# Fourteen of sixteen column groups of the second MLP product by the seven-product scheme, with sums made by GpSimd

## The chip, the cores and the metric

One core of one Trainium2 chip runs the whole kernel. The time is device time in microseconds, the median over runs; the profile is of one execution. The engines are named as the profile names them: PE is TensorE's matmul and PEld its weight load, DVE is VectorE, ACT ScalarE, POOL GpSimd, SP SyncE, on whose queue all of this kernel's loads and stores stand.

## The reference

One layer of an encoder on 512 tokens of 2048 features, all in float32. A projection feeds sixteen heads of two recurrent kinds (gated linear recurrence and gated delta rule), their output is projected back and added to x, and then comes the part that this change is about:

```python
h2 = rmsnorm(x, norm2_w[layer])
hid = jnp.square(jax.nn.relu(jnp.einsum("btd,df->btf", h2, w_mlp_in[layer])))
x = x + jnp.einsum("btf,fd->btd", hid, w_mlp_out[layer])
...
return rmsnorm(x, final_norm_w)
```

Here hid has 512 x 8192 elements and w_mlp_out 8192 x 2048. The last line but one is the second MLP product.

## The kernel before

**Precision.** Every float32 operand of a large product is split into a high part, rounded by ACT to the matmul's float32 format (`fp32r`), and a low part, the rest, subtracted by DVE. A product is then three matmuls (mm3, lines 103 to 106: high x high, high x low, low x high). So each tile of weights costs one ACT copy and one DVE subtraction before PE can use it.

**The second product (from line 1189 on).** The 64 row tiles (128 rows each) of w_mlp_out make four blocks of 16 (`FB`, `NB`), and each block is taken through four groups of 512 columns. A group has eight steps (`NK`); a step takes a pair of row tiles. After each group the result is added to x2, which lies in DRAM and is loaded before (`load_group`) and stored after (`store_group`), through one buffer on chip.

A *plain* group (`plain_group`, line 1254) does 2 row tiles x 4 token tiles x 3 = 24 matmuls of 512 columns per step. Its weights are 512 KB from DRAM into a raw buffer (three of them), one ACT copy, one DVE subtraction (lines 75 and 78).

A *fast* group (`fast_group`, line 1293) uses Strassen's scheme in Winograd's form: halves of the tokens, even and odd row tiles, halves of the columns, seven products of half the size for eight. That is 7 x 2 x 3 = 42 matmuls of 256 columns per step, in seven PSUM banks. `weights7` (line 1265) makes a step's weights: the load into a raw buffer, three sums of quarters into a tile of tag "T" (`quarters`, line 1200, two buffers; lines 1273 to 1275: one instruction 512 wide, two of 256), then two splits: b, 768 wide, from raw (lines 1277, 1278), and wh and wl, 1024 wide, from the sums (lines 1282, 1283; three buffers each). `finish_fast` (line 1310) adds the seven banks into x2: one ACT copy and nine DVE additions, of which the first six read a bank and the last three have both inputs on chip in SBUF.

**Left-hand sides.** For each pair of row tiles of a block the hidden activations come back from DRAM in two forms. `load_parts` (line 1211) loads 512 KB into a raw buffer and splits them into hidA, which plain and fast groups use. `load_sums` (line 1220) loads the same 512 KB once more, into a "T" buffer, makes the four sums of the scheme in place, each 256 wide (lines 1226 to 1229), and splits the tile into hidS, which fast groups alone use. There are eight buffers for parts and eight for sums, so those of the next block can be written only as the last group of this one gives them up.

**When they are made.** `todo` (lines 1332 to 1340) puts each load at a step of the program. Parts of block b at step kp + 6 (`LAG`) counted from the start of group 3 of the block before; sums of block b at the group ahead of the block's first fast group. `FAST` names the fast groups of each block: (2, 3) in blocks 0 to 2 and (1, 2) in block 3, eight of sixteen. So the program puts the sums of blocks 0 to 2 into plain group 1 and those of block 3 into plain group 0. The last group of the last block is written apart (lines 1359 to 1405) and is plain.

**Order.** PE's instructions stand in the order of the program (`manual_schedule`, line 265). For the other engines a scheduler sets a fixed order by priority ahead of the run, and each engine and the SP queue then work through it in that order; a waiting instruction holds up all that stand behind it on its engine.

GpSimd has little to do: powers and masks in the first phase, nothing in the second product but four small powers at the end.

Of the kernel before, what the change touches and what calls it, by code (L numbers as in the profile page):

```python
# [16 lines left out]
P = 128  # L17
# [15 lines left out]
def encoder_layer_kernel(ctx, tc, x, norm1_w, w_in, lb_fwd, lb_bwd, hg_norm_w, conv_w,  # L33
# [13 lines left out]
    def after(later, first):  # L47
        """issue order only"""
        tc.add_manual_dep(getattr(later, "ins", later), getattr(first, "ins", first).name,
                          mybir.DependencyInfo(mybir.DependencyClass.NoSync, mybir.DependencyReason.DATA),  # L50
                          reason="issue order")

    # ------------------------------------------------------------------ pools
# [17 lines left out]
    # ------------------------------------------------------------------ weights  # L71
# [11 lines left out]
    def load_cols(w, k0, c0, name):  # L83
        """[1024 rows of w from k-tile k0] x 128 columns -> [128, 8 k-tiles, 128]"""
# [9 lines left out]
    def load_rows(w, k0, c0, name):  # L94
        """[256 rows of w from k-tile k0] x 512 columns -> [128, 2 k-tiles, 512]"""
# [12 lines left out]
    def project(w, c0, rh, rl, name):  # L108
        """(columns c0..c0+127 of act @ w) transposed: PSUM [128 columns, 512 tokens]; four k-tiles per step"""
# [9 lines left out]
    def project_narrow(w, c0, width, rh, rl, name, between):  # L119
        """the same for a few columns; high and low parts of the weights side by side, their products to be added"""  # L120
# [20 lines left out]
    # ------------------------------------------------------------------ input rows  # L141
# [10 lines left out]
    # ------------------------------------------------------------------ constants  # L152
# [61 lines left out]
    # ------------------------------------------------------------------ first norm, transposed  # L214
# [3 lines left out]
    def tiles16(name):  # L218
        """sixteen [128, 512] tiles, four to a unit of 8 KB"""
# [5 lines left out]
    def rms_scale(ss, n, width, name, post=None):  # L225
        """(ss / width + eps) ** -0.5 for [128, n] sums of squares"""
# [43 lines left out]
    # ------------------------------------------------------------------ masks  # L270
    # rows are the partition index p, columns f
# [9 lines left out]
    def tri(dst, src, fill, lower, strict=False):  # L281
        """keep src where f >= p (upper) or f <= p (lower), else fill"""
# [21 lines left out]
    # ------------------------------------------------------------------ decays and betas of the delta rule  # L304
# [7 lines left out]
    def decays():  # L312
# [47 lines left out]
        # summation matrices, [r, t]: which g_r enter the sum of token t  # L360
# [29 lines left out]
    # ------------------------------------------------------------------ centred short convolution + silu  # L390
# [10 lines left out]
    # ------------------------------------------------------------------ delta rule, first pass: N = strict(beta k k^T decay)  # L401
# [13 lines left out]
    def decay_matrix(gb, wa, wb, mask, sign, h):  # L415
        """exp(sign * (gb - w + mask)), in place; w = wa / wb for the columns of a pair's first / second half"""
# [46 lines left out]
    # ------------------------------------------------------------------ delta rule: (I - M)^-1 of 128 blocks of 64 x 64  # L463
# [22 lines left out]
    # ------------------------------------------------------------------ shared end of a head: norm of o, transposed  # L486
    mixh = bp.tile([P, NH, T], F32, tag="B0", name="mixh")

    def head_norm(o, qcol, wcol, dst, name):
        """o [128 tokens, 4 x 128] (PSUM or SBUF) -> dst = (rmsnorm(o * qcol) * w) transposed"""  # L490
# [26 lines left out]
    # ------------------------------------------------------------------ HGRN2 head  # L517
# [14 lines left out]
    def hgrn_gates(h, d, pf, q):  # L532
        """decayed queries and keys of one direction, all [128 channels, 512 tokens]"""
# [31 lines left out]
    def hgrn_extend(h, r, size, dl, name):  # L565
        """decays of qi / ks reach over 2 * size tokens instead of size"""
# [11 lines left out]
    def hgrn_scores_32(h, r):  # L578
        """scores [s, t]: inside blocks of 32 tokens and between the two blocks of each 64"""
# [87 lines left out]
    # ------------------------------------------------------------------ delta rule, second pass  # L667
    def delta_second(h):
# [22 lines left out]
        # merge 64 -> 128  # L691
# [743 lines left out]
```

## Time and profile before

| | us |
|---|---|
| median of 3 runs (2541.36 to 2544.16) | 2541.64 |
| span of the profiled execution, first to last instruction | 2540.0 |
| second MLP product up to its last matmul, from 1856 | 675.3 |
| PE busy in the span | 2504.5 |
| DVE busy in the span | 1744.5 |
| ACT busy in the span | 1213.1 |
| POOL busy in the span | 64.9 |

The time of the profiled execution is known by its span alone; what lies around it shows in the median being 1.6 us longer. In a view that groups instructions a row is line, engine, operation, what it writes and reads, shapes, count | busy time, mean ns of one | idle time of the engine before them and what ended it. Busy time of PE counts matmuls whose ends are modelled and which overlap, so a step's time is read from stretches between starts, not from one matmul's duration. A name such as wl<-wsum,wh gives the tile written and those read, without buffer numbers.

### The profile page before, as it was taken

Reading aid. Unit: us, or ns where it says so; the run is one execution under the profiler, and the core shown is the slowest. Engines: PE = TensorE matmul, PEld = TensorE weight load, DVE = VectorE, ACT = ScalarE, POOL = GpSimd, SP = SyncE. Lnnn points to the kernel's source line nnn. Section 1 sums busy time; section 2 is a strip of 40 time slices with the busy share of each in tenths; the row PEclk is TensorE's granted clock in tenths of the full one; section 3 lists DMA queues with packets and bytes.
Section 4 is the critical chain, followed back from the end, with each engine's and each line's share of the span. In section 5 each row is a group of like instructions: output and inputs, shape, how many; then the busy total and the mean of one; then the engine's idle time right before and its main releaser. Section 6 shows DMA issues by size and latency. Waiting matters only on the chain.

```text
span 2540.0 us, 39593 instructions
## 1 busy us (share of the span) xinstructions
PE 2504.5 (99%) x16010; PEld 2236.5 (88%) x16010; DVE 1744.5 (69%) x2782; ACT 1213.1 (48%) x1768; POOL 64.9 (3%) x94
## 2 busy tenths in 40 slices
PE   7999999999999999999999999999999999999998
PEld 5888888887888888888899999999988989989897
DVE  5989995445545454444777777777767867868885
ACT  5564555563444443344655555555544433434443
POOL 2000000000000100000000000000000000000000
PEclk9999999999999999999999999999999999999999
DMA  5662223233333332433333344334375573754764
GB/s 159 176 171 75 75 75 114 83 101 88 108 98 94 103 101 67 166 125 124 127 132 125 129 151 136 125 126 150 111 237 191 184 248 134 264 191 167 245 217 168
DMA packets 339452, 359.50 MB, mean 142 GB/s; under 512 B 42898, under 2 KB 256052, under 8 KB 334148
## 3 DMA queue, kind: packets, MB, share of 16 engines
q1 hardware_dynamic: 339268, 356.96, 43.7%
q8 instruction: 126, 2.06, 0.3%
q14 instruction: 58, 0.48, 0.1%
HBM read 306.55 MB, written 50.36 MB: 141 GB/s over the span
## 4 chain that ended last, share of the span: by engine, by line
PE 88%; DMA 4%; DVE 4%; ACT 2%; issue 1%; SPq 0%; ACTq 0%; POOLq 0%; POOL 0%; DVEq 0%
PE mo L106 3%; PE mo L104 3%; PE mo L105 3%; PE p L104 3%; PE p L105 3%; PE p L106 3%; PE wo L104 2%; PE wo L106 2%; PE wo L105 2%; PE mc L104 2%; PE mc L106 2%; PE md L104 2%; PE md L106 2%; PE mc L105 2%; PE md L105 2%; PE ma L104 2%
## 5 line engine op out<-in xcount | busy, mean ns | idle before, releaser
L1099 ACT ACTIVATE wh<-s 128x1024 fp32r<-128x1024 f32 x128 | 135.8, 1061 | 130.2 <-PE mb L105 48.7
L105 PE MATMUL mo<-wl_mo,hidA 128*128 128x512 f32 x480 | 187.4, 390 | 1.8 <-DVE wl_mo L78 1.8
L104 PE MATMUL mo<-wh_mo,hidA 128*128 128x512 f32 x480 | 188.5, 393 | 0.7 <-DVE u L1316 0.3
L106 PE MATMUL mo<-wh_mo,hidA 128*128 128x512 f32 x480 | 188.2, 392 | 0.0
L1100 DVE TENSOR_TENSOR wl<-s,wh 128x1024 fp32r<-128x1024 f32 x128 | 156.6, 1223 | 36.7 <-ACT wh L1099 36.6
L1099 ACT ACTIVATE wh<-praw 128x1024 fp32r<-128x1024 f32 x96 | 101.9, 1061 | 148.5 <-PE mc L105 52.3
L1100 DVE TENSOR_TENSOR wl<-praw,wh 128x1024 fp32r<-128x1024 f32 x96 | 117.1, 1220 | 36.6 <-ACT wh L1099 36.4
L1277 ACT ACTIVATE wb<-raw 128x768 fp32r<-128x768 f32 x64 | 54.1, 845 | 133.3 <-issue 58.1
L105 PEld LDWEIGHTS mo<-wl_mo,hidA 128*128 128x128 f32 x480 | 90.1, 188 | 22.7 <-DVE wl_mo L78 3.1
L105 PE MATMUL p<-wl,hidS 128*128 128x256 f32 x384 | 108.3, 282 | 0.9 <-DVE wl L1283 0.9
L104 PE MATMUL p<-wh,hidS 128*128 128x256 f32 x384 | 108.4, 282 | 0.8 <-DVE x L1355 0.8
L104 PEld LDWEIGHTS mo<-wh_mo,hidA 128*128 128x128 f32 x480 | 90.2, 188 | 21.0 <-DVE x L1316 1.2
L106 PE MATMUL p<-wh,hidS 128*128 128x256 f32 x384 | 108.2, 282 | 0.0
L106 PEld LDWEIGHTS mo<-wh_mo,hidA 128*128 128x128 f32 x480 | 90.1, 188 | 19.7
L1092 DVE TENSOR_TENSOR s<-praw 128x1024 f32<-128x1024 f32 x64 | 78.4, 1225 | 36.3 <-DMA praw<-in_w_mlp_in_dram 35.2
L78 DVE TENSOR_TENSOR wl_wo<-raw_wo,wh_wo 128x1024 fp32r<-128x1024 f32 x32 | 39.2, 1225 | 92.1 <-ACT wh_wo L75 92.1
L104 PE MATMUL wo<-wh_wo,mh 128*128 128x512 f32 x256 | 100.1, 391 | 0.0
L78 DVE TENSOR_TENSOR wl_mo<-raw_mo,wh_mo 128x1024 fp32r<-128x1024 f32 x60 | 73.1, 1220 | 39.2 <-ACT wh_mo L75 39.0
L106 PE MATMUL wo<-wh_wo,ml 128*128 128x512 f32 x256 | 99.7, 389 | 0.0
L105 PE MATMUL wo<-wl_wo,mh 128*128 128x512 f32 x256 | 99.6, 389 | 0.0
L75 ACT ACTIVATE wh_mo<-raw_mo 128x1024 fp32r<-128x1024 f32 x60 | 62.8, 1052 | 66.6 <-PE mo L106 27.6
L1282 ACT ACTIVATE wh<-wsum 128x1024 fp32r<-128x1024 f32 x64 | 67.1, 1050 | 41.2 <-PE mo L106 25.1
(515 smaller groups left out, 8577.8 us busy)
## 6 DMA issues: line engine op xcount, KB each, us to landing
praw<-in_w_mlp_in_dram SPq DMA_DIRECT2D x64, 1024.0 KB, 8.5
raw<-in_w_mlp_out_dram SPq DMA_DIRECT2D x64, 512.0 KB, 4.0
raw_mo<-in_w_mlp_out_dram SPq DMA_DIRECT2D x60, 512.0 KB, 5.1
raw_wo<-in_w_out_dram SPq DMA_DIRECT2D x32, 512.0 KB, 3.6
hid_d<-r SPq DMA_DIRECT2D x64, 256.0 KB, 4.4
raw_h<-hid_d SPq DMA_DIRECT2D x32, 512.0 KB, 4.2
x<-x_d SPq DMA_DIRECT2D x16, 1024.0 KB, 7.1
sums<-hid_d SPq DMA_DIRECT2D x32, 512.0 KB, 4.7
```

The lines of the kernel that those rows point to most:

```text
L75: op = act.activation(wh, raw, AF.Copy)
L78: op = dve.tensor_tensor(wl, raw, wh.bitcast(F32), ALU.subtract)
L104: pe.matmul(ps, ah, bh, start=start, stop=False, skip_group_check=skip)
L105: pe.matmul(ps, ah, bl, start=False, stop=False, skip_group_check=skip)
L106: return pe.matmul(ps, al, bh, start=False, stop=stop, skip_group_check=skip)
L1092: dve.tensor_tensor(t, x0, x1, op)
L1099: act.activation(wh, src, AF.Copy)
L1100: dve.tensor_tensor(wl, src, wh.bitcast(F32), ALU.subtract)
L1277: act.activation(b[:, 0], r[:, 1:4], AF.Copy)
L1282: act.activation(wh, qf, AF.Copy)
```

## The change

Three things are changed, all in the second product:

- `FAST` names fourteen groups: (1, 2, 3), all four, all four, (0, 1, 2). Plain are left group 0 of block 0 and group 3 of block 3.
- The sums of a block are made at `SUM_LAG` = 4 steps after the start of group 3 of the block before, those of block 0 at the steps of its group 0.
- GpSimd makes the three weight sums of `weights7` and two of the four sums of `load_sums`; DVE keeps the two others and all splits.

```diff
-    FAST = ((2, 3), (2, 3), (2, 3), (1, 2))
+    FAST = ((1, 2, 3), (0, 1, 2, 3), (0, 1, 2, 3), (0, 1, 2))
+    SUM_LAG = 4
...
     def load_sums(fb, kp, first):
...
-        dve.tensor_tensor(q[:, 3], q[:, 1], q[:, 3], ALU.add)
+        pool.tensor_tensor(q[:, 3], q[:, 1], q[:, 3], ALU.add)
         dve.tensor_tensor(q[:, 1], q[:, 1], q[:, 0], ALU.subtract)
-        dve.tensor_tensor(q[:, 0], q[:, 3], q[:, 0], ALU.subtract)
+        pool.tensor_tensor(q[:, 0], q[:, 3], q[:, 0], ALU.subtract)
         dve.tensor_tensor(q[:, 2], q[:, 2], q[:, 0], ALU.subtract)
         split8(s, q)
...
     def weights7(fb, g, kp):
...
-        dve.tensor_tensor(q[:, 0:2], r[:, B12:B12 + 1].to_broadcast([P, 2, HT]), r[:, B11:B22 + 1], ALU.subtract)
-        dve.tensor_tensor(q[:, 2], r[:, B22], q[:, 0], ALU.subtract)
-        dve.tensor_tensor(q[:, 3], r[:, B21], q[:, 2], ALU.subtract)
+        pool.tensor_tensor(q[:, 0:2], r[:, B12:B12 + 1].to_broadcast([P, 2, HT]), r[:, B11:B22 + 1], ALU.subtract)
+        pool.tensor_tensor(q[:, 2], r[:, B22], q[:, 0], ALU.subtract)
+        pool.tensor_tensor(q[:, 3], r[:, B21], q[:, 2], ALU.subtract)
...
-            todo.setdefault((4 * b + FAST[b][0] - 1) * NK + kp, []).append((sums, load_sums, b, kp, b == 0 and kp >= 4))
+            at = kp if b == 0 else (4 * b - 1) * NK + kp + SUM_LAG
+            todo.setdefault(at, []).append((sums, load_sums, b, kp, b == 0 and kp >= 4))
```

In the changed kernel lines from 1198 on are one further down: the sums of `load_sums` are lines 1227 to 1230, the weight sums 1274 to 1276, the splits 1210, 1279 and 1284, the additions of a finish 1317.

The order shows what this moves at the join of block 0 and block 1. Names carry block, group and step, or block and row pair, ahead of a running tile number: wsum0_3_6 are the weight sums of block 0, group 3, step 6; wb and wl the low parts of its two splits; sums1_1 the sum tile of block 1, pair 1; hidS and hidA the splits of sums and parts. DVE before, in the last steps of fast group 3 of block 0:

```order
L1273 TENSOR_TENSOR wsum0_3_7_18867<-raw_0_3_7_18865 128x512
L1274 TENSOR_TENSOR wsum0_3_7_18867<-raw_0_3_7_18865,wsum0_3_7_18867 128x256
L1278 TENSOR_TENSOR wb0_3_6_18811<-raw_0_3_6_18805,wb0_3_6_18811 128x768
L1283 TENSOR_TENSOR wl_0_3_6_18815<-wsum0_3_6_18807,wh_0_3_6_18814 128x1024
L1275 TENSOR_TENSOR wsum0_3_7_18867<-raw_0_3_7_18865,wsum0_3_7_18867 128x256
L1209 TENSOR_TENSOR hidA1_0_18862<-raw_h1_0_18860,hidA1_0_18862 128x1024
L1278 TENSOR_TENSOR wb0_3_7_18871<-raw_0_3_7_18865,wb0_3_7_18871 128x768
L1283 TENSOR_TENSOR wl_0_3_7_18875<-wsum0_3_7_18867,wh_0_3_7_18874 128x1024
```

DVE in the changed kernel, in the same two steps and the first of the next block:

```order
L1279 TENSOR_TENSOR wb0_3_6_19041<-raw_0_3_6_19035,wb0_3_6_19041 128x768
L1228 TENSOR_TENSOR sums1_1_19027<-sums1_1_19027 128x256
L1230 TENSOR_TENSOR sums1_1_19027<-sums1_1_19027 128x256
L1284 TENSOR_TENSOR wl_0_3_6_19045<-wsum0_3_6_19037,wh_0_3_6_19044 128x1024
L1210 TENSOR_TENSOR hidS1_1_19026<-sums1_1_19027,hidS1_1_19026 128x1024
L1210 TENSOR_TENSOR hidA1_0_19092<-raw_h1_0_19090,hidA1_0_19092 128x1024
L1279 TENSOR_TENSOR wb0_3_7_19110<-raw_0_3_7_19104,wb0_3_7_19110 128x768
L1228 TENSOR_TENSOR sums1_2_19096<-sums1_2_19096 128x256
L1284 TENSOR_TENSOR wl_0_3_7_19114<-wsum0_3_7_19106,wh_0_3_7_19113 128x1024
L1230 TENSOR_TENSOR sums1_2_19096<-sums1_2_19096 128x256
L1210 TENSOR_TENSOR hidA1_1_19161<-raw_h1_1_19159,hidA1_1_19161 128x1024
L1210 TENSOR_TENSOR hidS1_2_19095<-sums1_2_19096,hidS1_2_19095 128x1024
```

The weight sums have left DVE; between the splits of one step's weights and the next stand two sums, the split of a sum tile and the split of a part. GpSimd in the changed kernel at this place, where it had nothing before:

```order
L1274 TENSOR_TENSOR wsum0_3_6_19037<-raw_0_3_6_19035 128x512
L1227 TENSOR_TENSOR sums1_1_19027<-sums1_1_19027 128x256
L1275 TENSOR_TENSOR wsum0_3_6_19037<-raw_0_3_6_19035,wsum0_3_6_19037 128x256
L1276 TENSOR_TENSOR wsum0_3_6_19037<-raw_0_3_6_19035,wsum0_3_6_19037 128x256
L1229 TENSOR_TENSOR sums1_1_19027<-sums1_1_19027 128x256
L1274 TENSOR_TENSOR wsum0_3_7_19106<-raw_0_3_7_19104 128x512
```

L1229 can start when DVE's L1228 of the same tile is done, and the next step's weight sums stand behind it. The SP queue in the changed kernel, from the load of step 6's weights on:

```order
L1270 DMA raw_0_3_6_19035<-in_w_mlp_out_dram 128x2x512
L1206 DMA raw_h1_0_19090<-hid_d_8722 128x2x512
L1206 DMA sums1_1_19027<-hid_d_8722 128x2x512
L1270 DMA raw_0_3_7_19104<-in_w_mlp_out_dram 128x2x512
L1206 DMA raw_h1_1_19159<-hid_d_8722 128x2x512
L1206 DMA sums1_2_19096<-hid_d_8722 128x2x512
L1270 DMA raw_1_0_0_19200<-in_w_mlp_out_dram 128x2x512
L1206 DMA raw_h1_2_19255<-hid_d_8722 128x2x512
```

Each load of weights stands behind the load of a sum tile. Before, group 3's own weights came ahead of the first sums, and at the join the queue read:

```order
L1269 DMA raw_0_3_7_18865<-in_w_mlp_out_dram 128x2x512
L1205 DMA raw_h1_1_18920<-hid_d_8722 128x2x512
L1205 DMA sums1_0_19261<-hid_d_8722 128x2x512
L98 DMA raw_mo1_0_0_18949<-in_w_mlp_out_dram 128x2x512
L1205 DMA raw_h1_2_18979<-hid_d_8722 128x2x512
L98 DMA raw_mo1_0_1_18984<-in_w_mlp_out_dram 128x2x512
L1205 DMA sums1_1_19300<-hid_d_8722 128x2x512
```

There the weights behind the sums were those of plain steps (raw_mo), which need no "T" buffer.

## The prediction

> **What bounds the kernel now.** I read the page's first part, then stretches of the second MLP product group by group, then PE's waits there.
>
> ```profile
> span 2540.0 us, 39593 instructions
> PE 2504.5 (99%) x16010; PEld 2236.5 (88%) x16010; DVE 1744.5 (69%) x2782; ACT 1213.1 (48%) x1768; POOL 64.9 (3%) x94
> ...
> 1856.01:1946.55 90.54, 88.69 (x386) 71.79 (x385) 58.18 (x81) 38.74 (x44) 0.00 (x0) 1.00 0.66 228
> ...
> 2025.90:2113.81 87.91, 87.91 (x386) 72.11 (x385) 61.19 (x84) 29.50 (x30) 0.00 (x0) 1.00 0.63 221
> 2113.81:2192.96 79.15, 79.15 (x674) 79.14 (x672) 64.65 (x89) 32.96 (x37) 0.00 (x0) 1.00 0.54 186
> ...
> 2360.42:2405.41 44.99, 44.53 (x194) 35.90 (x193) 40.45 (x58) 21.09 (x22) 0.00 (x0) 1.00 0.75 261
> ```
>
> The columns of a stretch are its length, then busy time of PE, PEld, DVE, ACT and POOL, the granted clock, the DMA share and GB/s. 1856 to 1947 is plain groups 0 and 1 of block 0, 2026 to 2114 the plain pair of block 1, 2114 to 2193 its fast pair, 2360 to 2405 plain group 0 of block 3, where eight parts and eight sums are prepared within one group. A plain group takes 87.91 / 2 = 43.96 us, a fast one 79.15 / 2 = 39.58, or 4.95 for each of its eight steps, with weight loads back to back (79.14 of 79.15). PE has almost nothing to wait for; all its waits from 1830 on are:
>
> ```profile
> PE mo L105 <- DVE wl_mo L78: 1.8, 2, 0.9
> PE p L105 <- DVE wl L1283: 0.9, 2, 0.7
> PE p L104 <- DVE x L1355: 0.8, 1, 0.8
> PE mo L104 <- DVE u L1316: 0.3, 1, 0.3
> PE mo L104 <- DVE x L1316: 0.2, 1, 0.2
> ```
>
> They come to 4.0 us. So TensorE bounds this stage, and relieving DVE by itself can gain 4 us at most.
>
> **The change, part by part.** *Six groups change form.* Each saves 43.96 - 39.58 = 4.38 us as long as its weights and sums arrive in time: 6 x 4.38 = **-26.3 us**. Everything else asks whether they do. What VectorE does in a fast pair:
>
> ```profile
> L1283 DVE TENSOR_TENSOR wl<-wsum,wh 128x1024 fp32r<-128x1024 f32 x14 | 17.1, 1223 | 0.4 <-ACT wh L1282 0.4
> L1278 DVE TENSOR_TENSOR wb<-raw,wb 128x768 fp32r<-128x768 f32 x13 | 12.4, 954 | 7.9 <-ACT wb L1277 7.9
> L1273 DVE TENSOR_TENSOR wsum<-raw 128x512 f32<-128x512 f32 x12 | 8.3, 690 | 1.6 <-DMA raw<-in_w_mlp_out_dram 1.4
> L1274 DVE TENSOR_TENSOR wsum<-raw,wsum 128x256 f32<-128x256 f32 x12 | 5.0, 423 | 0.3
> ...
> L1209 DVE TENSOR_TENSOR hidA<-raw_h,hidA 128x1024 fp32r<-128x1024 f32 x4 | 4.9, 1225 | 3.8 <-ACT hidA L1208 3.8
> ...
> L1316 DVE TENSOR_TENSOR x<-x,u 128x512 f32<-128x512 f32 x2 | 1.3, 683 | 0.0
> ...
> L1316 DVE TENSOR_TENSOR x<-x,u 128x1024 f32<-128x1024 f32 x1 | 1.2, 1216 | 0.0
> ...
> L1228 DVE TENSOR_TENSOR sums<-sums 128x256 f32<-128x256 f32 x2 | 0.8, 425 | 0.1
> ```
>
> And ScalarE's copies, the first half of every split:
>
> ```profile
> L1282 ACT ACTIVATE wh<-wsum 128x1024 fp32r<-128x1024 f32 x14 | 14.7, 1047 | 8.3 <-PE mo L106 4.4 <-DVE wsum L1275 3.8
> L1277 ACT ACTIVATE wb<-raw 128x768 fp32r<-128x768 f32 x13 | 11.0, 846 | 31.5 <-PE p L106 16.2 <-issue 15.3
> L1208 ACT ACTIVATE hidA<-raw_h 128x1024 fp32r<-128x1024 f32 x4 | 4.2, 1060 | 10.6 <-DMA raw_h<-hid_d 10.6
> ```
>
> A step's weights cost DVE 1.22 + 0.95 for the two splits and 0.69 + 2 x 0.42 = 1.53 for the sums. The sums go to GpSimd, 2.17 stay. A part (hidA) costs 1.22. A sum tile costs 4 x 0.42 + 1.22 before; two of its four additions move, 2.07 stay.
>
> *GpSimd's price.* The trace has no addition of this size on GpSimd. The nearest rows:
>
> ```profile
> L673 POOL MEMSET tf<- 64x256 f32 x8 | 2.5, 307 | 214.4 <-PE st L771 214.3
> L299 POOL MEMSET rst<- 128x512 f32 x1 | 0.5, 525 | 0.0
> L363 POOL COPY cm<-tris 128x128 f32<-128x128 f32 x1 | 0.3, 293 | 0.0
> ```
>
> Below, a fill, which reads nothing: 0.53 for 512 wide, 0.31 for 256, so 1.14 per step's weights and 0.61 per sum tile. Above, two copies, since an addition reads twice: 8 x 0.293 = 2.34 for 512, 1.17 for 256, so 4.69 and 2.34. I take one copy scaled by width, 2.34 and 1.17: a copy both reads and writes, and its fixed share, counted in at every scaling, leaves room for the second input. The Trainium skill (GPSIMD Engine Reference, 3.1) has 4497 ns for a 2048-wide fp32 addition; an estimate from that is about 1.12 for 512, 2.25 per step, which would leave the sum as it is.
>
> *Do the two engines work at the same time?* Two places of the first phase, DVE above GpSimd in each:
>
> ```profile
> 264.56 1.18 DVE L473 TENSOR_TENSOR prod<-Y 128x986 f32<-128x986 f32 x1
> 266.64 0.17 DVE L500 TENSOR_SCALAR orr_hg<-orr_hg 128x4 f32<-128x4 f32 x1 [0.90 <-POOL orr_hg L499]
> 264.73 1.87 POOL L499 TENSOR_TENSOR orr_hg<-orr_hg,mhalf 128x4 f32<-128x4 f32 x1 [54.66 <-DVE orr_hg L498]
> ...
> 606.23 0.69 DVE L705 TENSOR_TENSOR ksf<-tr_gk,gdec 128x512 f32<-128x512 f32 x1
> 606.40 1.01 POOL L499 TENSOR_TENSOR orr_hg<-orr_hg,mhalf 128x4 f32<-128x4 f32 x1 [62.74 <-DVE orr_hg L498]
> ```
>
> The same power on GpSimd takes 1.01 us beside a DVE instruction with one input in PSUM, but 1.87 beside one with both inputs in SBUF: it ends 0.86 after that one's end (264.56 + 1.18 = 265.74). GpSimd waits until such a DVE instruction is over. Every split, every sum and the last additions of a finish (x<-x,u) are of that kind. The other direction, a DVE instruction that arrives second, stands here for a tiny read only:
>
> ```profile
> 83.20 0.28 DVE L420 SCALAR_TENSOR_TENSOR gb<-gb,cum,pos_lo 128x64 f32<-128x64 f32 x1 [0.43 <-DMA gb<-gc_rows]
> 82.77 1.04 POOL L710 TENSOR_TENSOR cols<-cols,phalf 128x4 f32<-128x4 f32 x1 [55.52 <-DVE rk L444]
> ```
>
> DVE, both inputs in SBUF, ran inside the power unhindered, but GpSimd had presumably read its four columns by then. An addition reads for its whole length, so I expect DVE to wait there, and add up the times of both. The Trainium skill (SBUF — State Buffer, "Who interferes with whom") states that whichever of the two starts first holds the shared port for the whole instruction and the other fully blocks; the first pair of rows agrees, the L420 row does not for "the whole instruction". By that rule the sum is the one made here; read by the L420 row alone it is the second rival's.
>
> *A steady fast step* then takes of the port 2.17 + 2.34, and an eighth of a finish, (2 x 0.68 + 1.22) / 8 = 0.32: 4.84 of 4.95. That just fits, with no room to regain a lead; for imperfect turns I add 1 us to each of the eight fast groups away from the joins: **+8** (0 to 32, half a microsecond in each of 64 steps).
>
> *The three joins of blocks* (group 3 of a block, group 0 of the next, all fast now; before, parts and sums were made mostly in plain groups, whose steps need 1.22 of DVE). Over about eight steps a part and a sum tile are added to each step's weights: 2.17 + 2.34 + 1.22 + 2.07 + 1.17 = 8.97 us of port against 4.95 of TensorE. 8 x 8.97 + 2.6 for the finish - 8 x 4.95 = 34.8. Weights are at most two steps ahead (three buffers): 9.9 us to spend, fully at the first join, hardly at the next two. About 25 + 33 + 32 = **+90**.
>
> At the joins three things queue behind one another: GpSimd's second addition of a sum tile waits for DVE's subtraction, behind which the next weights' additions stand; on SP a sum's load waits for its T buffer, and the weight loads stand behind it. What stays under 4.95 even there: ACT with 1.05 + 0.85 + 2 x 1.06 = 4.0 per step, and the transfers, three loads of 512 KB per step or 318 GB/s, where the 2360 stretch moved 261 at a share of 0.75.
>
> *Block 0, group 0* now prepares sums beside parts, as the 2360 stretch did in 44.99, one over a plain group; in exchange the old sums stage leaves group 1 (90.54 - 87.91 = 2.6 lost there). **0** (-2 to +6).
>
> Sum: -26.3 + 8 + 90 = +71.7. On the profiled span that is 2611.7; the median of the runs is 1.6 above that span (2541.64 against 2540.0): **2613 us**.
>
> **The rivals.** *1. The engines overlap and tiles turn over at row times: faster.* A T buffer holds a sum tile for its load and work:
>
> ```profile
> sums<-hid_d SPq DMA_DIRECT2D x32, 512.0 KB, 4.7
> ...
> L1226 DVE TENSOR_TENSOR sums<-sums x8: 417/422/426, 1878.8 to 1919.3; 128x256 f32<-128x256 f32 x8
> ```
>
> 4.7 + 2.0 (two additions on each engine) + 1.06 + 1.22 = 9.0, and a weight tile 2.34 + 1.05 + 1.22 = 4.6. Two tiles a step over two buffers: 6.8, so a join costs 8 x 1.85 - 9.9 = 4.9, three 15; 2541.6 - 26.3 + 15 = 2530, or 2528 without block 0's old stall. For it: DVE has time, 65 of 79 us in a fast pair, and gets relief. Against: the 264 us rows. It wins if a GpSimd addition beside a split stays under about 1.2 us and the split at 1.22.
>
> *2. DVE does not wait, but the two T buffers bind.* The L1226 row is eight sum tiles in a plain group: seven intervals in 40.5 us, 5.8 each, so a buffer is held 11.6, not 9.0. (11.6 + 4.6) / 2 = 8.1 a step; a join costs 8 x 3.15 - 9.9 = 15.3, three 46: 2541.6 + 20 = 2561.
>
> *3. GpSimd at two copies.* 4.69 puts every step at 7.2: 112 x 2.24 = +251, joins 3 x 8 x 5.6 = +135: about 2900. Against: a fill of 512 is 0.53.
>
> *The change not doing what it says:* no; PE's list of instructions grows from 14628 to 15492, by 864, which is 6 groups x 8 steps x (42 - 24) matmuls.
>
> **How the numbers follow.** Forecast (port shared by turns) 0.60, own range 2561 (a fill's price, where rival 2's buffers bind) to 2672 (10% lost in turns at the joins, +126, and +32 in the steady steps). Rival 1 0.13, rival 2 0.20, rival 3 0.07. A measurement of this kernel can tell about 0.2%, 5 us, from no change. From 2540 to 2675 leaves out rivals 1 and 3, 0.20 in all. Faster 0.14 (rival 1 and a little of rival 2's edge), same 0.04, slower 0.82.
>
> **What would show it.** In the new profile: GpSimd rows L1274 to L1276 well above 0.6 to 1.2 us and split rows L1284 above 1.22, both stretched by waiting for each other; PE waiting for wl and hidS at the three joins, some 30 us each; groups 1 and 2 near 40 us. It is wrong if additions and splits keep their lengths side by side (rivals 1, 2), if the loss is spread evenly over all fast steps (rival 3), or if PE's waits at the joins are single microseconds.

## The result, and the profile after

The changed kernel takes **2643.2 us** (median of 4 runs, 2641.7 to 2645.43) against 2542.8 (4 runs, 2541.36 to 2544.16) for the kernel before, run beside it on the same chip: a ratio of **1.040** (95% interval 1.0388 to 1.0413). That is 100 us slower; the prediction said 71 us slower, 2613, with a range from 2540 to 2675.

The first part of the page of the changed kernel:

```profile
span 2643.7 us, 41834 instructions
...
PE 2524.8 (96%) x16874; PEld 2293.7 (87%) x16874; DVE 1774.2 (67%) x2604; ACT 1254.2 (47%) x1822; POOL 565.1 (21%) x494
```

PE's share falls from 99 to 96%. DVE has 178 instructions fewer and is busy for longer (1774 against 1744): the first sign that its instructions are stretched. The first seven groups of the stage, one by one (columns as in the prediction; a stretch is one group): plain group 0 and fast groups 1 to 3 of block 0, then groups 0 to 2 of block 1, which begins at 2050.37:

```profile
1856.19:1912.86 56.67, 49.42 (x195) 38.53 (x193) 37.22 (x41) 26.95 (x30) 20.84 (x22) 0.91 0.67 232
1912.86:1958.56 45.70, 42.73 (x338) 42.52 (x337) 26.78 (x25) 18.36 (x22) 34.74 (x30) 0.93 0.47 150
1958.56:1998.22 39.66, 39.66 (x338) 39.66 (x337) 27.86 (x25) 17.71 (x22) 31.74 (x25) 1.00 0.47 160
1998.22:2050.37 52.15, 43.35 (x338) 42.54 (x336) 34.78 (x38) 22.91 (x28) 29.07 (x25) 0.90 0.53 185
2050.37:2113.93 63.56, 47.85 (x336) 45.58 (x336) 44.59 (x44) 24.97 (x28) 45.88 (x37) 0.89 0.52 173
2113.93:2155.81 41.88, 41.48 (x336) 41.27 (x337) 32.34 (x29) 15.75 (x18) 35.88 (x27) 0.96 0.49 163
2155.81:2195.38 39.57, 39.57 (x338) 39.57 (x337) 29.07 (x25) 15.19 (x18) 32.07 (x25) 1.00 0.47 160
```

Groups 2 (the third and the last row) run at TensorE's own 39.6: there nothing is lost. At the join of blocks 0 and 1, group 3 takes 52.15, group 0 of the next block 63.56 and group 1 still 41.88: 12.6 + 24.0 + 2.3 = 38.9 over three times 39.57. The other two joins cost 39.5 and 39.6 by the same reading (51.79, 64.44, 41.98 and 51.85, 64.43, 42.01), so the three make **118**. Block 0 starts with 56.67 and 45.70, 18.8 over a plain and a fast group.

The sum closes. The stretch from the first to the last matmul of the second product is 778.9 long, 675.3 before: +103.7, which is the whole difference of the spans (2643.7 - 2540.0). It is -26.3 for the six changed groups, +118 at the joins, and +12 in block 0 (18.8, less the 7.0 by which the stage before exceeded the bare time of its groups, 8 x 43.96 + 8 x 39.58 = 668.3).

PE's waits from 1850 on, where before all of them came to 4.0:

```profile
PE p L104 <- ACT wh L1283: 29.6, 13, 4.1
PE p L104 <- ACT u L1319: 26.9, 6, 6.2
PE p L105 <- DVE wl L1284: 18.9, 21, 1.3
PE mo L104 <- ACT hidA L1209: 3.4, 1, 3.4
PE p L104 <- DVE x L1357: 3.0, 1, 3.0
```

All rows together are 87 us; the rest of the loss is matmuls at half clock (see the dummy matmuls below). PE waits for the two halves that the weights' sums are split into (wh, wl), and for u, ACT's copy of the first bank in a finish. At the first join u stands in ACT's queue behind the split of a sum tile, for which ACT waits in its turn:

```profile
2048.78 1.06 ACT L1209 ACTIVATE hidS<-sums 128x1024 fp32r<-128x1024 f32 x1 [1.60 <-DVE sums L1230]
2049.74 0.58 ACT L1319 ACTIVATE u<-p 128x512 f32<-128x512 f32 x1
```

GpSimd's three additions of a step, and DVE's splits of the weights, over the stage:

```profile
L1274 POOL TENSOR_TENSOR wsum<-raw 128x512 f32<-128x512 f32 x112 | 183.2, 1636 | 138.2 <-DVE wl L1284 79.5 <-DVE hidS L1210 57.8 <-DMA raw<-in_w_mlp_out_dram 0.8
L1275 POOL TENSOR_TENSOR wsum<-raw,wsum 128x256 f32<-128x256 f32 x112 | 138.4, 1236 | 8.3
L1276 POOL TENSOR_TENSOR wsum<-raw,wsum 128x256 f32<-128x256 f32 x112 | 119.2, 1064 | 8.8
```

```profile
L1284 DVE TENSOR_TENSOR wl<-wsum,wh 128x1024 fp32r<-128x1024 f32 x112 | 162.8, 1453 | 54.7 <-ACT wh L1283 54.3
L1279 DVE TENSOR_TENSOR wb<-raw,wb 128x768 fp32r<-128x768 f32 x112 | 138.7, 1239 | 72.3 <-ACT wb L1278 72.1
```

DVE's splits were 1223 and 954 before and are 1453 and 1239 now. GpSimd's 256-wide additions take 0.71 at the least and 1.24 or 1.06 in the mean. How they stretch each other can be read in a steady stretch, group 2 of block 1, DVE first, then GpSimd:

```profile
2162.31 0.94 DVE L1279 TENSOR_TENSOR wb<-raw,wb 128x768 fp32r<-128x768 f32 x1
2163.18 2.33 DVE L1284 TENSOR_TENSOR wl<-wsum,wh 128x1024 fp32r<-128x1024 f32 x1
```

```profile
2162.46 1.97 POOL L1274 TENSOR_TENSOR wsum<-raw 128x512 f32<-128x512 f32 x1 [5.02 <-DVE wl L1284]
2164.51 1.61 POOL L1275 TENSOR_TENSOR wsum<-raw,wsum 128x256 f32<-128x256 f32 x1
```

Follow the ends. wb ends at 2163.25. GpSimd's first addition, begun inside it, ends at 2164.43, 1.18 later. DVE's wl, begun inside that one, takes 2.33 in place of 1.22 and ends at 2165.51, 1.08 after GpSimd's end. GpSimd's second addition, begun inside wl, ends at 2166.12, 0.61 later. So each waits for the other, in both directions, and what an addition keeps from DVE is 1.18 for 512 wide and 0.61 for 256: the prices taken were 1.17 and 0.59. The Trainium skill (SBUF — State Buffer, "Who interferes with whom") says this of the two engines in both directions; these rows agree, the new one being a DVE instruction with two SBUF inputs that came second and took 2.33 for 1.22.

### The profile page after: what moved, and what is told of

The parts are those of the page before. It is cut to its first block, busy times and chain, and to the rows that moved or that the text cites. A ratio compares the mean times of both kernels' runs of the same rounds, so it can differ in the third digit from the quotient of the medians.

```text
span 2643.7 us, 41834 instructions
## 1 busy us (share of the span) xinstructions
PE 2524.8 (96%) x16874; PEld 2293.7 (87%) x16874; DVE 1774.2 (67%) x2604; ACT 1254.2 (47%) x1822; POOL 565.1 (21%) x494
## 4 chain that ended last, share of the span: by engine, by line
PE 81%; POOL 7%; DVE 5%; issue 3%; ACT 2%; DMA 2%; SPq 0%; ACTq 0%; POOLq 0%; DVEq 0%
PE p L104 4%; PE p L106 4%; PE p L105 4%; PE mc L104 2%; PE mc L106 2%; PE mc L105 2%; PE md L106 2%; PE md L104 2%; POOL wsum L1274 2%; PE md L105 2%; PE ma L104 2%; PE wo L104 2%; PE wo L105 2%; PE wo L106 2%; PE ma L106 2%
## 5 line engine op out<-in xcount | busy, mean ns | idle before, releaser
L104 PE MATMUL p<-wh,hidS 128*128 128x256 f32 x672 | 202.6, 301 | 33.8 <-ACT wh L1283 29.6
L105 PE MATMUL p<-wl,hidS 128*128 128x256 f32 x672 | 202.8, 302 | 18.9 <-DVE wl L1284 18.9
L1274 POOL TENSOR_TENSOR wsum<-raw 128x512 f32<-128x512 f32 x112 | 183.2, 1636 | 138.2 <-DVE wl L1284 79.5
L106 PE MATMUL p<-wh,hidS 128*128 128x256 f32 x672 | 199.7, 297 | 0.0
L1284 DVE TENSOR_TENSOR wl<-wsum,wh 128x1024 fp32r<-128x1024 f32 x112 | 162.8, 1453 | 54.7 <-ACT wh L1283 54.3
L1283 ACT ACTIVATE wh<-wsum 128x1024 fp32r<-128x1024 f32 x112 | 118.4, 1057 | 169.6 <-POOL wsum L1276 169.1
L1279 DVE TENSOR_TENSOR wb<-raw,wb 128x768 fp32r<-128x768 f32 x112 | 138.7, 1239 | 72.3 <-ACT wb L1278 72.1
L1100 DVE TENSOR_TENSOR wl<-s,wh 128x1024 fp32r<-128x1024 f32 x128 | 156.5, 1223 | 34.0 <-ACT wh L1099 33.8
L104 PEld LDWEIGHTS p<-wh,hidS 128*128 128x128 f32 x672 | 138.2, 206 | 38.4 <-ACT wh L1283 32.7
L105 PEld LDWEIGHTS p<-wl,hidS 128*128 128x128 f32 x672 | 138.6, 206 | 23.5 <-DVE wl L1284 23.5
L104 PE MATMUL p<-wb,hidA 128*128 128x256 f32 x448 | 129.2, 288 | 26.9 <-ACT u L1319 26.9
L1275 POOL TENSOR_TENSOR wsum<-raw,wsum 128x256 f32<-128x256 f32 x112 | 138.4, 1236 | 8.3
L106 PEld LDWEIGHTS p<-wh,hidS 128*128 128x128 f32 x672 | 139.0, 207 | 0.0
L105 PE MATMUL p<-wb,hidA 128*128 128x256 f32 x448 | 128.7, 287 | 0.0
L106 PE MATMUL p<-wb,hidA 128*128 128x256 f32 x448 | 127.9, 285 | 0.0
L1276 POOL TENSOR_TENSOR wsum<-raw,wsum 128x256 f32<-128x256 f32 x112 | 119.2, 1064 | 8.8
```

Of the source, the lines that this page charges most:

```text
L104: pe.matmul(ps, ah, bh, start=start, stop=False, skip_group_check=skip)
L105: pe.matmul(ps, ah, bl, start=False, stop=False, skip_group_check=skip)
L106: return pe.matmul(ps, al, bh, start=False, stop=stop, skip_group_check=skip)
L1100: dve.tensor_tensor(wl, src, wh.bitcast(F32), ALU.subtract)
L1274: pool.tensor_tensor(q[:, 0:2], r[:, B12:B12 + 1].to_broadcast([P, 2, HT]), r[:, B11:B22 + 1], ALU.subtract)
L1275: pool.tensor_tensor(q[:, 2], r[:, B22], q[:, 0], ALU.subtract)
```

## The experiments

Theories, as the expectations name them. **A**: one port, used by turns; GpSimd's additions cost their time on it. **B**: the two T buffers, and the order of the queues through them, bind. **C**: GpSimd relieves DVE, which would be worse off alone. **D**: TensorE's half clock after long pauses costs a part of the loss by itself.

### All sums on DVE, fourteen groups fast

```diff
-        pool.tensor_tensor(q[:, 3], q[:, 1], q[:, 3], ALU.add)
+        dve.tensor_tensor(q[:, 3], q[:, 1], q[:, 3], ALU.add)
...
-        pool.tensor_tensor(q[:, 0:2], r[:, B12:B12 + 1].to_broadcast([P, 2, HT]), r[:, B11:B22 + 1], ALU.subtract)
+        dve.tensor_tensor(q[:, 0:2], r[:, B12:B12 + 1].to_broadcast([P, 2, HT]), r[:, B11:B22 + 1], ALU.subtract)
```

(and the other three additions alike)

> Fourteen fast groups as in the changed kernel, but all sums made by VectorE again. Theory A (VectorE and GpSimd take the shared port by turns): at a join a step then needs 2.17 + 1.53 + 1.22 + 2.92 = 7.84 us of it instead of 8.97, over TensorE's 4.95, so 0.72 of the changed kernel's loss of 137 us over its floor stays: about 2605. Theory B (the two T buffers and the order of the queues bind, the port does not): a weight tile is held 3.8 us instead of 4.6 beside a sum tile's 9.0, 6% less: about 2630. Theory C (GpSimd does relieve VectorE, and VectorE alone would be worse): above 2650.

Measured: 2600.65 (2598.22 to 2602.82), 1.0236 of before (1.0219 to 1.0253). Theory A had expected about 2605. GpSimd's share of the change costs 42 us, and theory C falls. But 59 us stay without GpSimd. Group 0 of block 1 in this kernel:

```profile
2038.45:2101.20 62.75, 48.03 (x338) 46.13 (x337) 59.35 (x90) 27.72 (x30) 0.00 (x0) 0.86 0.60 201
```

DVE is busy for 59.35 of 62.75: with parts, sums and weights' sums in one group of 39.6, DVE alone is overbooked. Its instructions have their old lengths (wl 1222).

### Fills in place of GpSimd's additions

```diff
-        pool.tensor_tensor(q[:, 3], q[:, 1], q[:, 3], ALU.add)
+        [pool.memset(q[:, 3], 0.5) for _ in range(2)]
...
-        pool.tensor_tensor(q[:, 0:2], r[:, B12:B12 + 1].to_broadcast([P, 2, HT]), r[:, B11:B22 + 1], ALU.subtract)
+        [pool.memset(q[:, 0:2], 0.5) for _ in range(2)]
```

> The changed kernel with each of GpSimd's five additions replaced by two fills of the same region with a constant: GpSimd writes for about as long (1.05 us for 512 columns, 0.61 for 256) but reads nothing, so the sums are left out. All waits, buffers and queues stay, except that the fill of the first weight sum no longer waits for its load. Theory A: VectorE's splits fall back to 0.95 and 1.22 us and a join step needs 5.46 us of VectorE, nearly covered by the lead: 2520 to 2550. Theory B: the tiles turn over as before: 2610 to 2645.

GpSimd's sums are left out in this kernel.

Measured: 2585.28 (one run), between the two expectations. The splits on DVE are back at their old lengths beside busy fills:

```profile
L1284 DVE TENSOR_TENSOR wl<-wsum,wh 128x1024 fp32r<-128x1024 f32 x112 | 136.9, 1223 | 29.2 <-ACT wh L1283 29.0
L1279 DVE TENSOR_TENSOR wb<-raw,wb 128x768 fp32r<-128x768 f32 x112 | 107.0, 955 | 150.5 <-ACT wb L1278 150.5
```

So taking GpSimd off the port while it keeps two instructions per addition (0.53 and 0.31 each) gives back 58 us, and 43 over before stay that are not GpSimd's share of the port. Two other things differ a little: two fills take 1.05 where an addition alone takes 1.29, and the first fill does not wait for its load, for which GpSimd waited 0.8 us in all in the changed kernel (the L1274 row above). Where these 43 are shows at the first join, DVE and then GpSimd:

```profile
2036.93 2.42 DVE L1317 TENSOR_TENSOR x<-x,u 128x512 f32<-128x512 f32 x3
2039.28 1.22 DVE L1210 TENSOR_TENSOR hidS<-sums,hidS 128x1024 fp32r<-128x1024 f32 x1
2040.41 1.22 DVE L1284 TENSOR_TENSOR wl<-wsum,wh 128x1024 fp32r<-128x1024 f32 x1
```

```profile
2032.36 0.68 POOL L1229 MEMSET sums<- 128x256 f32 x2 [0.32 <-DVE sums L1228]
2041.74 0.52 POOL L1274 MEMSET wsum<- 128x512 f32 x1 [8.71 <-DVE wl L1284]
```

GpSimd stands 8.71 us for a T buffer. Both are held, one by a sum tile (hidS), one by a step's weights (wl), and the two subtractions that would free them stand behind a finish in DVE's order. That finish began when group 3's banks were complete and has priority in the schedule.

### A third T buffer, paid with a b buffer

```diff
-        return p4.tile([P, 4, HT], F32, tag="T", name=name, bufs=2)
+        return p4.tile([P, 4, HT], F32, tag="T", name=name, bufs=3)
...
-        b = p4.tile([P, 2, 3, HT], F32R, tag="b", name="wb" + n, bufs=3)
+        b = p4.tile([P, 2, 3, HT], F32R, tag="b", name="wb" + n, bufs=2)
```

The third T buffer takes the room of a b buffer, so a second kernel has the lost b buffer alone, as the one to compare with.

> The changed kernel with three T buffers instead of two; to make room, the b tiles of the weights have two buffers instead of three. Theory A: the port is as full as before, 2630 to 2655. Theory B: (9.0 + 4.6) / 3 = 4.5 us per step, less than TensorE's 4.95, so the joins cost almost nothing: 2540 to 2575.

> The control to the three T buffers: the changed kernel with two b buffers and nothing else changed. Both theories: 2640 to 2660, so that the run with three T buffers is compared with this one.

Measured: 2658.28 with three T, 2681.33 without (one run each). The third T buffer is worth 23 us there, far from the 80 to 100 that B wanted as the whole cause. B is a part. A missed the first by 3 us over its upper end, and both theories missed the second (2640 to 2660): the lost b buffer costs 38, so the best that a third buffer could do with both in full is not known from these.

### The T buffers for the activations' sums alone

The kernel with fills, with the weights' sums left out:

```diff
-        q = quarters("wsum" + n)
-        [pool.memset(q[:, 0:2], 0.5) for _ in range(2)]
-        [pool.memset(q[:, 2], 0.5) for _ in range(2)]
-        [pool.memset(q[:, 3], 0.5) for _ in range(2)]
+        q = r
```

> The kernel with two fills for each GpSimd addition, and the weights' sums left out altogether: wh and wl are split from the raw weights, so that a T buffer is used by the sums of activations alone (fills and DVE's subtractions, as there). Leaves out the sums of the weights and half of those of the activations. Against the 2585 of the kernel with fills: theory B (weights' sums and activations' sums turn over in two T buffers) expects the rest of the loss to go, 2515 to 2545; if the rest is DVE's splits and the finish at the joins, it stays, 2570 to 2590.

Measured: 2538.42 (one run). 47 us of the rest are gone, as B expected. Group 0 of block 1, in the kernel with fills and then in this one:

```profile
2032.28:2089.83 57.55, 44.77 (x338) 43.51 (x337) 43.11 (x51) 26.80 (x30) 27.36 (x84) 0.88 0.63 209
```

```profile
2028.63:2074.79 46.16, 43.03 (x337) 41.71 (x338) 39.26 (x46) 23.30 (x26) 4.87 (x16) 0.96 0.76 256
```

It takes 46.16 for 57.55; DVE does the same splits and the same finish in both. So it is not DVE's work that holds the join of the kernel with fills, but the way of the weights through GpSimd and the T buffers. The experiment takes both away at once (no T buffer and no fill between a load and its split); which of the two weighs more it does not say. The 8.71 above points to the buffer.

Together: of the changed kernel's 2643, 58 us go with GpSimd's additions on the port and 47 more with the weights' way through the T buffers. That split holds for this order: no run takes the weights out of the T buffers while the additions stay on the port, so what the T buffers alone are worth there is not known. The 2538 that are left are 22 over 2516.5, which is the kernel before less 26.3.

### The weights' sums alone on GpSimd, and the activations' alone

```diff
-        pool.tensor_tensor(q[:, 3], q[:, 1], q[:, 3], ALU.add)
+        dve.tensor_tensor(q[:, 3], q[:, 1], q[:, 3], ALU.add)
...
-        pool.tensor_tensor(q[:, 0], q[:, 3], q[:, 0], ALU.subtract)
+        dve.tensor_tensor(q[:, 0], q[:, 3], q[:, 0], ALU.subtract)
```

(in load_sums for the one kernel; the three of weights7 for the other)

> The changed kernel with the weights' sums alone on GpSimd; the activations' sums are all on DVE again. It stands between the changed kernel (2643) and the one with all sums on DVE (2601). Theory A (shared port, prices held): at a join a step's weights cost the port 2.34 on GpSimd against 1.53 on DVE, 0.81 more, a sum tile 1.17 against 0.84, 0.33 more, so seven tenths of the 42 us belong to the weights: 2628 to 2635. A rival, that the chain through a sum tile, which goes from GpSimd to DVE and back twice, holds up DVE's queue: nearly all of the 42 is gone, 2600 to 2615.

> The changed kernel with its two additions for each sum tile of the activations alone on GpSimd; the weights' sums are on DVE again. Theory A: three tenths of the 42 us, 2608 to 2618. The rival, the chain between the two engines: 2628 to 2645.

Measured (one run each): 2640.01 with the weights' sums on GpSimd, 2610.81 with the activations'. Against 2600.65 with all on DVE that is +39 and +10, and the rival, the chain of a sum tile between the two engines, falls: it wanted it the other way round. The two come to 49 for the 42 of both together, so they do not simply add. Theory A had the second right (2608 to 2618) and missed the first by 5 us (2628 to 2635). The weights' sums weigh more than their share of the port: they also stand between a load and its split on the way to PE. By how much of either, these runs do not tell.

### Sums sooner

```diff
-    SUM_LAG = 4
+    SUM_LAG = 0
```

> The changed kernel with SUM_LAG 0 instead of 4: sums of the next block are made from the first step of group 3 on, so that sums and parts overlap in two steps instead of six. Theory A: the same port time is spread over the 14 or 15 steps instead of ten, 16 steps need 16 x 4.51 + 8 x 4.46 + 2.6 = 110 us against 79, less the lead of 10: 21 us of waiting per join instead of 25 to 29, and fewer long pauses: 2615 to 2635. Theory B: sums and weights still share two T buffers: 8.1 us a step for eight steps, 2625 to 2645. If the short lead were the cause: below 2590.

Measured: 2674.71 (one run), 31 slower than the changed kernel; every expectation missed, and none had it slower by more than 2 us. In group 3 of a block, now 66 to 68 long, GpSimd's next weights wait each time for a sum tile:

```profile
2214.84 1.91 POOL L1274 TENSOR_TENSOR wsum<-raw 128x512 f32<-128x512 f32 x1 [1.68 <-DVE hidS L1210]
...
2221.91 1.95 POOL L1274 TENSOR_TENSOR wsum<-raw 128x512 f32<-128x512 f32 x1 [3.56 <-DVE hidS L1210]
```

and a sum tile keeps its T buffer until PE gives up a hidS buffer of the block before:

```profile
2209.28 1.06 ACT L1209 ACTIVATE hidS<-sums 128x1024 fp32r<-128x1024 f32 x1 [4.35 <-PE p L106]
```

A sum that is begun ahead of its buffer does no work sooner; it holds a T buffer, the copy holds ACT, and the weights stand behind. That is argued from these rows; no run undoes it by itself.

### Dummy matmuls in PE's pauses

36 matmuls of 256 columns into a free bank behind the last product of a block's group 3, and 24 behind the first product at each of two steps of the next group 0:

```diff
+    def fill_pause(count, a, b):
+        ps = pbank("idle")
+        for k in range(count):
+            pe.matmul(ps[:, 0:HT], a, b, start=True, stop=True)
...
+                if fb > 0 and g == 0 and kp in (2, 4) and i == 1:
+                    fill_pause(24, l[:, 0, n, 0:P], wh)
+                if fb < NB - 1 and g == 3 and kp == NK - 1 and i == ORDER[6]:
+                    fill_pause(36, l[:, 0, n, 0:P], wh)
```

> The changed kernel, with matmuls into a spare PSUM bank put where TensorE pauses longest: 36 of 256 columns (about 4.1 us) at the end of group 3 of blocks 0 to 2, 24 (about 2.7 us) in steps 2 and 4 of group 0 of blocks 1 to 3, behind the first product. The pauses there are 6.0 to 6.4, 4.3 and 4.1 us, so the added matmuls should fit into them. Theory D (part of the loss is the clock, granted at one half for 3.4 or 6.8 us after a pause): nine such periods are avoided or halved, 1.7 to 3.4 us each: 2613 to 2628. If the clock costs nothing, or the halved periods stay: 2643 to 2650. If the added matmuls are not hidden: up to 2672.

What it asks: in the changed kernel PE's longest pauses are followed by slow matmuls. The pause of the first join, and the two stretches after it:

```profile
2044.38 0.28 PE L106 MATMUL p<-wh,hidA 128*128 128x256 f32 x1
2050.37 0.58 PE L104 MATMUL p<-wb,hidA 128*128 128x256 f32 x1 [5.71 <-ACT u L1319]
```

```profile
2050.40:2053.80 3.40, 3.40 (x15) 3.39 (x16) 3.40 (x5) 0.87 (x1) 2.47 (x3) 0.50 0.28 109
2053.80:2057.00 3.20, 3.20 (x29) 3.20 (x28) 3.20 (x6) 1.79 (x2) 1.02 (x2) 0.97 0.46 154
```

At a granted clock of 0.50, 15 matmuls go into 3.40 us, and 29 into 3.20 after it. Over the stage PE is busy for 692 where the bare time of the groups is 642: 50 us of slower matmuls, beside the 87 of waiting.

Measured: 2643.87 (2640.78 to 2646.81), 1.0396 of before (1.0382 to 1.0411): no gain, though the mean clock rises from 0.979 to 0.989. The granted clock of the stage is 0.97 for 0.94, so about half of the half-clock time is gone. PE is busy for 706 of 776 there, some 29 of it with the added matmuls: its own work takes about 15 us less than the 692, and its waits, the added matmuls counted in, come to 100 instead of 87. So D falls for the half that went: a faster PE only waits longer for the next weights. For the other half no run tells.

### Eleven fast groups, sums in a plain group 0

```diff
-    FAST = ((1, 2, 3), (0, 1, 2, 3), (0, 1, 2, 3), (0, 1, 2))
+    FAST = ((1, 2, 3), (1, 2, 3), (1, 2, 3), (1, 2))
...
-            at = kp if b == 0 else (4 * b - 1) * NK + kp + SUM_LAG
+            at = 4 * b * NK + kp
```

One kernel with all sums on DVE, one with GpSimd's share as in the change.

> Eleven fast groups, (1, 2, 3) in blocks 0 to 2 and (1, 2) in block 3, all sums by VectorE, and the sums of each block made during its plain group 0, where no weight needs a T buffer. Theory A: VectorE, about 50 us of work in each group 0 of 44 us, spills a little into group 1: three groups more by 4.38 us, and 2 to 4 us lost at each of the first three blocks: 2531 to 2541. If the spill is as costly as a join of the changed kernel: above 2560.

> The same eleven fast groups, with the weight sums and half of the activations' sums on GpSimd as in the changed kernel. Theory A: in group 0 a plain step needs 1.22 + 1.22 + 2.07 + 1.17 = 5.68 us of the port against 5.50 of TensorE, and in the fast groups 4.84 against 4.95: it just fits, 2532 to 2548. Theory C (GpSimd relieves VectorE): below the run with VectorE alone.

Measured: 2549.47 on DVE (2546.83 to 2551.6 in 10 runs, ratio 1.0027, 1.0017 to 1.0036) and 2571.79 with GpSimd (2570.93 to 2574.07, ratio 1.0114, 1.0101 to 1.0128). GpSimd costs again, 22 us, with no fast join at all, and C falls a second time. A missed both, by 8 and by 24 us over its upper ends. In the first, groups 0 and 1 of block 0 take 52.1 + 48.3 where the kernel before has 44.1 + 46.5. The other blocks lose 3 to 5 each (44.0 + 42.2, 45.2 + 43.3, 45.4 + 42.8 against 83.5). In the second, the first step of group 1 takes 11.3 to 14.7 in blocks 1 to 3, where it takes 7.2 to 8.7 in the first; what holds it there was not tried.

### Ten fast groups on DVE

The kernel before, with block 0 left as it is:

```diff
-    FAST = ((2, 3), (2, 3), (2, 3), (1, 2))
+    FAST = ((2, 3), (1, 2, 3), (1, 2, 3), (1, 2))
```

> The kernel before (all sums on DVE) with ten fast groups, (2, 3), (1, 2, 3), (1, 2, 3), (1, 2): block 0 as before, blocks 1 and 2 as in the run with eleven. Two groups change form, 2 x 4.38 = -8.8; in that run the pairs of groups 0 and 1 of blocks 1 and 2 lasted 86.3 and 88.6 against 43.96 + 39.58 = 83.5, so 2.8 and 5.1 come back. Theory A (what DVE can supply sets a join): 2542.8 - 8.8 + 2.8 + 5.1 = 2542, from 2537 to 2545. If the excess of the run with eleven came from block 0 alone: 2534 to 2536. Theory B (two T buffers bind as soon as sums and weights' sums share a stretch): 2545 to 2555.

Measured: 2537.23 (2535.38 to 2542.65 in 11 runs) against 2542.73 before on the same chip (15 runs): a ratio of 0.9979 (0.9970 to 0.9988). **This beats both kernels**, the one before by 5.5 us, or 0.2%: clear of the noise of these runs, though small. It lies at the lower edge of A's range. Groups 0 and 1 of block 1:

```profile
2023.11:2068.19 45.08, 44.52 (x194) 35.91 (x193) 42.16 (x60) 21.94 (x22) 0.00 (x0) 1.00 0.74 262
2068.19:2109.04 40.85, 39.95 (x337) 39.68 (x336) 36.95 (x55) 15.62 (x18) 0.00 (x0) 1.00 0.53 178
```

DVE is busy for 42.16 of 45.08: a plain group just takes the parts and sums of a block. These two groups and those of block 2 (44.17 + 42.93) take 2.4 and 3.6 over the 83.5, so the excess did not come from block 0 alone. In the kernel with eleven, block 0 had 16.9 of it and the other three 12.2 together.

## Why the prediction was right, and where its sizes were off

- **TensorE bounds, six groups give -26.3: right.** Steady fast groups stand at 39.57 as before.
- **GpSimd's price, one copy scaled by width: right in size, by luck in its reason.** 1.18 and 0.61 held, 1.17 and 0.59 taken. That a copy's fixed share, multiplied by four, stands for an addition's second input is a coincidence of sizes as far as these runs show. A fill's price and two copies were both wrong; rival 3 is out (no loss in steady groups). Alone, the 512-wide addition shows 1.29 at the least, the 256-wide 0.71, so a little of each is not on the port. The Trainium skill's figure (GPSIMD Engine Reference, 3.1), scaled to 512 wide, gave an estimate of 1.12; the trace's 1.29 alone and 1.18 held lie above it.
- **By turns, in both directions: right.** Splits are 1453 and 1239 for 1223 and 954. With that, rival 2's condition that DVE does not wait falls, and so does rival 1's (an addition beside a split under 1.2, the split at 1.22). What rival 2 said of the T buffers came true beside the turns: with the port's part taken out (fills), 47 us went when the weights' sums left the T buffers.
- **Steady step, 4.84 of 4.95 and +8: the 4.84 fits, imperfect turns cost 0.** Of the eight fast groups that the prediction put here, the four groups 2 lost nothing. The four groups 1 lost 13 (6.1 in block 0, 2.3 to 2.4 behind each join), nearly all of it in their first step, as a rest of what stands ahead of them; below it is counted there.
- **Joins, +90: right in place and kind, 28 too small.** Of the 28, 21 lie in groups 3 and 0, and 7 in the groups 1 behind them. Two things were mis-sized. The lead of 9.9 us that the three weight buffers were to give did not show: the first join costs 38.9, the others 39.5 and 39.6, where the working had 25, 33 and 32. Without a lead it gives 34.8 each, 104 for three. The other 14 the sum had no term for; turns through the T buffers and the queues are the likely cause, and no run measures them by themselves.

  The same working without a lead can be held against other runs, by groups 3 and 0 of each join over twice 39.57. In the changed kernel it gives 34.8, and they cost 36.6, 37.1 and 37.1. With all sums on DVE it gives 8 x 7.84 + 2.6 - 8 x 4.95 = 25.7, and they cost 25.9, 23.0 and 23.9. With fills, and the T buffers for the activations alone, it gives 8 x 5.46 + 2.6 - 8 x 4.95 = 6.7, and they cost 7.7, 6.7 and 6.6. With fills and the weights' sums in the T buffers it gives 6.7 as well, but they cost 18.1, 23.4 and 21.5. So a second limit stands under the first, at some 20 us a join; the prediction had it as rival 2 alone, for an engine that does not wait, at 15.3 with the lead taken off. That a sum of the port alone came as near as it did is in part luck: by these figures the port was the longer of the two limits here.

  The changed kernel's first join shows one such turn, DVE, GpSimd and ACT one after the other:

```profile
2055.13 2.42 DVE L1317 TENSOR_TENSOR x<-x,u 128x512 f32<-128x512 f32 x3
2057.47 0.41 DVE L1228 TENSOR_TENSOR sums<-sums 128x256 f32<-128x256 f32 x1
...
2062.00 1.22 DVE L1210 TENSOR_TENSOR hidS<-sums,hidS 128x1024 fp32r<-128x1024 f32 x1
```

```profile
2051.17 1.31 POOL L1274 TENSOR_TENSOR wsum<-raw 128x512 f32<-128x512 f32 x1 [2.89 <-DVE hidS L1210]
...
2054.07 0.75 POOL L1227 TENSOR_TENSOR sums<-sums 128x256 f32<-128x256 f32 x1
2057.97 1.65 POOL L1229 TENSOR_TENSOR sums<-sums 128x256 f32<-128x256 f32 x1 [3.14 <-DVE sums L1228]
2063.29 2.17 POOL L1274 TENSOR_TENSOR wsum<-raw 128x512 f32<-128x512 f32 x1 [3.68 <-DVE hidS L1210]
```

```profile
2067.10 1.06 ACT L1283 ACTIVATE wh<-wsum 128x1024 fp32r<-128x1024 f32 x1 [5.93 <-POOL wsum L1276]
```

  A sum tile is begun on GpSimd at 2054.07, waits for DVE's subtraction behind a finish until 2057.47, is split at 2062.00, and only then has GpSimd a T buffer for the next weights: 12.1 us from one step's weights to the next (2051.17 to 2063.29). ACT then stands idle for 5.93 until their sums are made. The prediction named this queue and gave it no price. The other queue that it named, weight loads behind a sum's load on SP, cost little: GpSimd waited 0.8 us for weights from DRAM in the whole stage.
- **Block 0, group 0 at 0 (-2 to +6): failed.** Groups 0 and 1 take 102.4, 12 more than the 90.5 before, though one of them is now a fast group. Group 0 alone takes 56.67 for the 44.99 of the model. The model was the 2360 stretch, plain group 0 of block 3. That group began at 2360.42 with two sum tiles made; the kernel before has their first additions on DVE here:

```profile
2350.31 0.42 DVE L1226 TENSOR_TENSOR sums<-sums 128x256 f32<-128x256 f32 x1
...
2356.80 0.43 DVE L1226 TENSOR_TENSOR sums<-sums 128x256 f32<-128x256 f32 x1 [0.18 <-DMA sums<-hid_d]
```

  In the changed kernel block 0's first comes 9 us after the start of its group (1856.19), on GpSimd:

```profile
1865.24 0.73 POOL L1227 TENSOR_TENSOR sums<-sums 128x256 f32<-128x256 f32 x1 [776.26 <-DMA sums<-hid_d]
```

  So two tiles' work that the model had ahead of the group falls into it here. GpSimd is not the cause of the larger part of group 0's rise: it lasts 52.3 with all sums on DVE, 52.2 with fills, 52.2 with the T buffers free of weights, 52.1 with eleven groups on DVE. The other 4 go with the activations' additions on GpSimd (55.8 with these alone there, 52.2 with the weights' alone, one run each). That the late start alone makes the 8 us is argued; no run moves it. The kernel with eleven on DVE, which makes a block's sums in its group 0 each time, bears it out that block 0 is the exception: 52.1 there, 44.0 to 45.4 in the other blocks. Group 1's rise (48.8, 45.3, 40.6 in the first three kernels named) goes with the way of its weights through the T buffers.

- **The signs: in part.** The rows of GpSimd and of the splits are stretched as foretold, and groups 2 stand near 40 us. PE's waits at a join come to some 25 us, not 30, and they are for wh, u and wl; it never waits for hidS. The other 14 of a join's 39 are matmuls at half clock, for which the prediction had no term.

Sum: +28 at the joins, +12 in block 0, -8 in the steady groups: +32 on 2611.7, the span that was forecast, gives the 2643.7 of the trace.

## What to carry to other kernels

Work that is moved to an engine sharing a port with the one to be relieved has to be costed on the port: the step's sums took 1.53 us of DVE and take 1.18 + 2 x 0.61 = 2.40 of the port on GpSimd, and relief became a loss of 42 us. A change that removes the slack groups (the plain ones, where parts and sums were made) has to be summed for the place where all of that work meets, not on an average: the groups 2 lost nothing, the joins 118 us, and the start of the stage 12. And where several kinds of work turn over in one pair of buffers, price the longest holder including what stands ahead of its last reader; the lead that the buffer count seemed to allow did not show here.

## What the runs showed of the hardware

- GpSimd's additions and DVE's instructions with both inputs in SBUF hold each other up in both directions, by 1.18 and 0.61 us per addition of 512 and 256 columns; fills on GpSimd leave DVE's splits at 1223 and 955 ns.
- After a pause of TensorE of 5.71 us the granted clock was 0.50 for the next 3.40 us. The Trainium skill (TensorE: Matmul & The Clock Gate, Part 1) speaks of a half clock after an idle window of about 3.4 us; the trace agrees for this pause. It also shows the half clock after shorter ones: a pause of 2.99 us ended at 2113.93, and from 2115.41 to 2118.82 the granted clock was 0.50. Unexpected was that filling such pauses brought nothing (2643.87 against 2643.2): where another engine set the pace, the slow matmuls that went came back as waits.
